# Two narrow query tiles of a causal attention transposed one behind the other in heads 0 to 6

## The chip, the cores and the metric

The kernel runs on one core of a Trainium2 chip. The metric is the device time in microseconds (us) of one execution. TensorE multiplies matrices, VectorE and ScalarE work on rows of 128 partitions, GpSimd and SyncE do little here but small vector work and the issue of transfers. In the profile's rows they are PE (its weight loads are PEld), DVE, ACT, POOL and SP.

## The reference, cut to what matters

The program is a two-layer trunk over 1024 frames of width 1024, in fp32, causal in chunks of 64 frames. Layer 1 is multi-scale retention. Layer 2, in which the change lies, is a latent attention of eight heads: queries, keys and values are projected from shared latents, each head takes

```python
scores = q_nope @ k_nope.T + q_rope @ k_rope.T     # 1024 x 1024, chunk-causal
p      = softmax(masked scores)
o      = p @ v                                     # 128 wide a head
h      = h + rmsnorm_post((silu(gate) * o) @ W_out)
```

Only the order in which the kernel works through query tiles is touched by the change; what is computed stays the same.

## The kernel before, in words

**Products.** TensorE multiplies fp32 data as two halves, so each product is three matmuls (mm3, L232 to L234: low by high, high by low, high by high). A result that is to be multiplied again is split when it leaves the accumulator: ScalarE copies the high part (L238), VectorE subtracts it from the result (L239). Each split frees its accumulator bank only when both have read it. There are two banks "acc" for products, two "r" for transposes, and two double banks "S" for scores.

**Tiles.** A head has eight query tiles i of 128 rows; tile i sees the first (i + 1) x 128 keys. They are taken from wide to narrow pairs: step 0 and 1 take b = 3 (tiles 6 and 7), steps 6 and 7 take b = 0 (tiles 0 and 1); qi is the place in the pair, i = 2b + qi. `score` (L1349) does ten matmuls, five for each piece of at most 512 keys (five in all up to 512), then VectorE writes the mask (L1376) and finds the maximum (L1379), ScalarE does the exponential with the row sum (L1382), and VectorE the reciprocal (L1383) and the product with it (L1384).

**Two steps late.** A tile is finished two steps after its scoring (LAG = 2): `finish` (L1387) first computes the values of the pair that is complete (`values`, L1419: 3 matmuls of 256 columns for each block of 128 keys, then a product with the gate on VectorE, L1430), and then transposes the tile's probabilities block by block on TensorE into an "r" bank (L1412) and splits them into pT. Only when the second tile of a pair (qi = 1) is transposed can the pair's values be computed, and that happens at the head of the next `finish`.

**Fill.** Between scoring and finishing, the next head's projections are placed as filler (`head_projections`, L1227): k blocks of 6, q blocks of 9 matmuls, and, for each even head, rotary query blocks with their rotation (L1280 to L1283 and L1292 on VectorE, eight transfers of L1288 on SyncE's queue, L1291 on ScalarE) and eight v blocks. So the odd heads 1, 3 and 5 carry the rotations of the heads 2, 4 and 6. In head 7 the filler is the output projection (its matmuls read thi, tlo, uhi and ulo; VectorE makes ulo, 128x1024, by the same split). How much filler a step takes is set by a count of columns: `done` sums what the step's own matmuls will stream, and filler is added until it reaches the step's share. A scheduler then sets the final order on each engine by estimated times.

**Blocks.** The probabilities p, their transposes pT and most other tiles come from one pool of 51 blocks of 128x1024 fp32 (`heap`), and a block that is given back is reused by the next that asks.

Of the kernel before, what the change touches and what calls it, by code (L numbers as in the profile page):

```python
# [18 lines left out]
P = 128  # L19
# [6 lines left out]
NH = 8  # L26
# [3 lines left out]
LAG = 2  # L30
# [22 lines left out]
class Units:  # L53
# [75 lines left out]
    def next(self):  # L129
        if not self.ready:  # L130
            self.prep()
        u = self.ready.popleft()
        self.fill()

        if self.at < len(self.order):
            n = self.pairs.index(self.order[self.at][0]) + 2
            while self.n_fetched < min(n, len(self.pairs)):
                self.fetch()
        return u
# [58 lines left out]
class Trunk:  # L198
# [1096 lines left out]
    def attention(self):  # L1295
        nc, I, heap = self.nc, self.I, self.heap
        self.heads = {}
        self.rq = []
        for half in range(2):
            r = heap.get("rq")  # L1300
            nc.sync.dma_start(r.rearrange("p (a t) -> p a t", a=2),
                              I["ropeq"][:, :, half * HALF:(half + 1) * HALF])
            self.rq.append(r)
        for _ in self.head_projections(0):
            pass
        self.pv = None
        open_tiles = deque()

        own = sum(5 * max(i + 1, 2) * P + (i + 1) * 2 * P + (i // 2 + 1) * 3 * 256 for i in range(NT))
        head, pair = 10 * 3 * HALF, 6 * 3 * HALF + 16 * 3 * 256  # L1310
        for h in range(NH):
            done = 0
            if h + 1 < NH:
                fill = self.head_projections(h + 1)
                share = (own + head + (pair if h % 2 else 0)) / 8
            else:
                self.prepare_out()
                fill = self.out_units()
                next(fill)
                share = (own + 32 * 3 * HALF) / 8  # L1320
            for step in range(8):
                b, qi = 3 - step // 2, step % 2
                s = self.score(h, b, qi)
                done += 5 * max(2 * b + qi + 1, 2) * P
                if self.pv is not None:
                    done += 6 * (self.pv[1] + 1) * 256
                if len(open_tiles) == LAG:
                    done += (2 * open_tiles[0][1] + open_tiles[0][2] + 1) * 2 * P
                while done < (step + 1.1) * share:
                    cost = next(fill, 0)  # L1330
                    if not cost:
                        break
                    done += cost
                if len(open_tiles) == LAG:
                    self.finish(open_tiles.popleft())
                open_tiles.append(s)
            if h + 1 < NH:
                for _ in fill:
                    pass
        self.scored = True  # L1340
        while open_tiles:
            self.finish(open_tiles.popleft())
            for _ in range(8):
                next(fill, 0)
        self.finish(None)
        for _ in fill:
            pass

    def score(self, h, b, qi):  # L1349

        nc, heap = self.nc, self.heap
        st = self.heads[h]
        mm = nc.tensor.matmul
        (qh, ql), (kh, kl), qr = st["q"], st["k"], st["pair"]["qr"][h % 2]
        rh, rl = self.krT
        i = 2 * b + qi
        qs = slice(i * P, (i + 1) * P)
        w = (i + 1) * P
        pieces = 1 if w <= HALF else 2
        used = w // pieces  # L1360
        n = max(used, 256)
        sc = self.bank("S", (P, 2, HALF))
        for c in range(pieces):
            ks = slice(c * n, (c + 1) * n)
            o = sc[:, c, :n]
            mm(o, ql[:, qs], kh[:, ks], start=True, stop=False)  # L1366
            mm(o, qh[:, qs], kl[:, ks], start=False, stop=False)  # L1367
            mm(o, qh[:, qs], kh[:, ks], start=False, stop=False)  # L1368

            mm(o, qr[:, qs], rl[:, ks], start=False, stop=False)  # L1370
            mm(o, qr[:, qs], rh[:, ks], start=False, stop=True)  # L1371
        if i == 1:
            heap.free(*st["q"], *st["k"])
            if h % 2:
                heap.free(*st["pair"]["qr"])
        nc.vector.memset(sc[0:64, pieces - 1, used - 64:used], -BIG)  # L1376
        view = sc[:, :pieces, :used]
        nm = self.small([P, 1], "nm", bufs=2)
        nc.vector.tensor_reduce(out=nm, in_=view, op=ALU.max, axis=AX.XY, negate=True)  # L1379
        p = heap.get("p")  # L1380
        sm = self.small([P, 1], "sm", bufs=2)
        nc.scalar.activation(p[:, :w].rearrange("p (a b) -> p a b", a=pieces), view, AF.Exp, bias=nm, accum_out=sm)  # L1382
        nc.vector.reciprocal(sm, sm)  # L1383
        nc.vector.tensor_scalar_mul(p[:, :w], p[:, :w], sm)  # L1384
        return h, b, qi, p
# [304 lines left out]
```

## Time and profile before

| | |
|---|---|
| runs of the kernel | 1257.58, 1258.1, 1259.8 us (median 1258.1) |
| the profiled execution | 1257.16 us, its span 1255.4 us |
| mean granted TensorE clock | 0.996 |
| TensorE, VectorE, ScalarE busy | 98 %, 83 %, 52 % of the span |
| attention (first score to the last head's last tile) | about 893 to 1205 us |

The profiled execution's time is 1.76 us more than its span, and 0.94 us below the median of the runs. A matmul's row has its start and its length; because matmuls overlap in the pipeline, the pace of TensorE is read from start to start, and a stall is a step from one start to the next that is longer than the pace of that kind of matmul. The table of busy times cannot show such stalls of a few tenths.

### The profile page before, as it was taken

The numbers are of one execution on the slowest core, as the hardware profiler recorded it, in microseconds if no ns is written. First come the engines' busy times: TensorE is split into PE (matmuls) and PEld (weight loads), VectorE is DVE, ScalarE is ACT, GpSimd is POOL, SyncE is SP. The second block draws the span as 40 slices with busy tenths as digits, with TensorE's granted clock in tenths as the row PEclk, the third lists the DMA queues.
The fourth block names the chain that finished last, engine by engine and source line by source line (L and its number), as shares of the span: only waits on it lengthen the run. The fifth ranks groups of instructions, "written<-read, shape, count | busy, mean of one in ns | idle before, by whom it ended". The sixth has DMA issues, their size and how long they took to land. (4 is left out here: it accounts for less than half of the span.)

```text
span 1255.4 us, 17688 instructions
## 1 busy us (share of the span) xinstructions
PE 1228.2 (98%) x6520; PEld 1058.8 (84%) x6520; DVE 1041.9 (83%) x1871; ACT 652.2 (52%) x1154; POOL 69.7 (6%) x86
## 2 busy tenths in 40 slices
PE   6999999999999999999999999999999999999997
PEld 5888888888888888888888789978888989898875
DVE  6878778898898988999998884675689888879787
ACT  7632125555564565655644867574354545545432
POOL 2000000000000000000000332100000000000001
PEclk9999999999999999999999999999999999999999
DMA  9248991232222322239799641032501010102454
GB/s 352 89 156 318 326 323 51 76 112 70 87 68 86 120 68 70 68 124 349 264 348 379 211 143 51 1 134 82 203 12 49 22 35 26 45 28 102 170 199 168
DMA packets 59640, 175.25 MB, mean 140 GB/s; under 512 B 7073, under 2 KB 16289, under 8 KB 59553
## 3 DMA queue, kind: packets, MB, share of 16 engines
q1 hardware_dynamic: 59552, 174.12, 39.3%
q8 instruction: 51, 0.84, 0.3%
q14 instruction: 37, 0.30, 0.1%
HBM read 124.81 MB, written 45.09 MB: 135 GB/s over the span
## 5 line engine op out<-in xcount | busy, mean ns | idle before, releaser
L232 PE MATMUL acc<-xhi,unit 128*128 128x512 f32 x560 | 220.5, 394 | 2.7 <-DVE u L414 2.3
L233 PE MATMUL acc<-xlo,unit 128*128 128x512 f32 x560 | 219.2, 391 | 0.0
L234 PE MATMUL acc<-xhi,unit 128*128 128x512 f32 x560 | 218.4, 390 | 0.0
L232 PEld LDWEIGHTS acc<-xhi,unit 128*128 128x128 f32 x560 | 105.4, 188 | 23.5 <-DVE u L414 2.7
L234 PEld LDWEIGHTS acc<-xhi,unit 128*128 128x128 f32 x560 | 105.2, 188 | 21.8
L233 PEld LDWEIGHTS acc<-xlo,unit 128*128 128x128 f32 x560 | 105.4, 188 | 19.3
L232 PE MATMUL acc<-vhi,xlo 128*128 128x512 f32 x224 | 88.9, 397 | 1.0 <-DVE xlo L239 1.0
L234 PE MATMUL acc<-vhi,xhi 128*128 128x512 f32 x224 | 88.0, 393 | 0.0
L233 PE MATMUL acc<-vlo,xhi 128*128 128x512 f32 x224 | 88.0, 393 | 0.0
L1382 ACT ACTIVATE p<-S,nm 128x896 f32<-128x896 f32 (+3 forms) x64 | 47.4, 741 | 63.5 <-DVE nm L1379 60.5
L238 ACT ACTIVATE unit<-wsum 128x512 fp32r<-128x512 f32 x80 | 50.4, 631 | 54.1 <-PE acc L234 44.7
L238 ACT ACTIVATE unit<-wraw 128x512 fp32r<-128x512 f32 x60 | 37.7, 630 | 56.3 <-DMA wraw<-in_w_in_a_dram 24.0
L238 ACT ACTIVATE vhi<-wv 128x1024 fp32r<-128x1024 f32 x28 | 29.3, 1060 | 64.8 <-PE acc L233 15.3
L239 DVE TENSOR_TENSOR unit<-wsum,unit 128x512 fp32r<-128x512 f32 x80 | 54.4, 684 | 8.5 <-ACT unit L238 8.4
L238 ACT ACTIVATE pT<-r 128x512 fp32r<-128x512 f32 (+2 forms) x96 | 44.4, 489 | 31.6 <-PE r L1412 31.4
L239 DVE TENSOR_TENSOR pT<-r,pT 128x512 fp32r<-128x512 f32 (+2 forms) x96 | 50.8, 550 | 6.1 <-ACT pT L238 5.8
L786 POOL TENSOR_TENSOR rg<-rg,mhalf 128x2 f32<-128x2 f32 x32 | 24.6, 768 | 547.3 <-DVE rg L785 527.1
L232 PEld LDWEIGHTS acc<-vhi,xlo 128*128 128x128 f32 x224 | 42.6, 190 | 10.0 <-DVE xlo L239 1.4
L238 ACT ACTIVATE thi<-wl 128x1024 fp32r<-128x1024 f32 x36 | 37.9, 1059 | 25.1 <-PE r L234 5.2
L232 PE MATMUL acc<-thi,slo 128*128 128x512 f32 x128 | 50.7, 397 | 0.0
L233 PE MATMUL acc<-tlo,shi 128*128 128x512 f32 x128 | 50.4, 395 | 0.1
L234 PE MATMUL acc<-thi,shi 128*128 128x512 f32 x128 | 50.4, 394 | 0.0
(327 smaller groups left out, 3467.2 us busy)
## 6 DMA issues: line engine op xcount, KB each, us to landing
wraw<-in_w_in_a_dram SPq DMA_DIRECT2D x32, 512.0 KB, 4.1
wv<-in_w_v_dram SPq DMA_DIRECT2D x28, 512.0 KB, 6.5
wl<-in_w_out_a_dram SPq DMA_DIRECT2D x28, 512.0 KB, 6.7
yl<-yd SPq DMA_DIRECT2D x28, 512.0 KB, 6.0
vd<-vo SPq DMA_DIRECT2D x32, 256.0 KB, 2.9
td<-wl SPq DMA_DIRECT2D x16, 512.0 KB, 3.3
vt<-vd SPq DMA_DIRECT2D x16, 512.0 KB, 3.2
yd<-yT SPq DMA_DIRECT2D x16, 512.0 KB, 4.7
```

The lines of the kernel that those rows point to most:

```text
L232: mm(ps, lhs[1], rhs[0], start=first, stop=False, skip_group_check=more)
L233: mm(ps, lhs[0], rhs[1], start=False, stop=False, skip_group_check=more)
L234: mm(ps, lhs[0], rhs[0], start=False, stop=last, skip_group_check=more)
L238: self.nc.scalar.activation(hi, src, AF.Copy)
L239: self.nc.vector.tensor_sub(lo, src, hi.bitcast(F32))
L786: nc.gpsimd.tensor_tensor(out=rg, in0=rg, in1=self.mhalf[:, 0:1].to_broadcast([P, 2]), op=ALU.pow)
L1382: nc.scalar.activation(p[:, :w].rearrange("p (a b) -> p a b", a=pieces), view, AF.Exp, bias=nm, accum_out=sm)
```

## The change

A function `due` says how many of the open tiles are finished in a step. In heads 0 to 6 the first tile (qi = 0) of the pairs b = 1 and b = 0 is held back one step, so three tiles are open, and in the next step both tiles of the pair are finished one directly behind the other. The count `done` sums over all tiles that are due. The values of pair b = 2 move from the sixth step to the seventh (counted from 0), those of b = 1 from step 0 to step 1 of the next head; in the step in which a tile is held, the pending values stay pending and are counted in `done` in both steps.

```diff
@@ -1324,14 +1324,15 @@
                 done += 5 * max(2 * b + qi + 1, 2) * P
                 if self.pv is not None:
                     done += 6 * (self.pv[1] + 1) * 256
-                if len(open_tiles) == LAG:
-                    done += (2 * open_tiles[0][1] + open_tiles[0][2] + 1) * 2 * P
+                due = self.due(open_tiles)
+                for o in list(open_tiles)[:due]:
+                    done += (2 * o[1] + o[2] + 1) * 2 * P
                 while done < (step + 1.1) * share:
                     cost = next(fill, 0)
                     if not cost:
                         break
                     done += cost
-                if len(open_tiles) == LAG:
+                for _ in range(due):
                     self.finish(open_tiles.popleft())
                 open_tiles.append(s)
             if h + 1 < NH:
@@ -1345,6 +1346,14 @@
         self.finish(None)
         for _ in fill:
             pass
+
+    def due(self, tiles):
+
+        if len(tiles) < LAG:
+            return 0
+        if len(tiles) == LAG and tiles[0][0] < NH - 1 and tiles[0][1] < 2 and tiles[0][2] == 0:
+            return 0
+        return len(tiles) - LAG + 1
 
     def score(self, h, b, qi):
 
```

The number of instructions on each engine stays the same. Lines behind the new function stand 9 lower than before (L1412 becomes L1421, L1430 becomes L1439).

On TensorE at the passage from an even head to an odd one, before: the end of a pair's values (acc_9795 from pT), then the one transpose of tile 0 (r_9812), then the scores of the widest tile, nine matmuls of a rotary query block (cqT by wlo and whi), the two transposes of tile 1 (r_9863), and the 320-column scores.

```order
4752 L234 MATMUL acc_9795<-pT_9713,v_9257 128x256
4753 L1412 MATMUL r_9812<-ident_136,p_9685 128x128
4754 L1366 MATMUL S_9816<-kT_9441,qT_9572 128x512
...
4763 L1371 MATMUL S_9816<-krT_7082,qr_8960 128x512
4764 L232 MATMUL acc_9853<-cqT_7523,wlo_9438 128x512
...
4772 L234 MATMUL acc_9853<-cqT_7525,whi_9437 128x512
4773 L1412 MATMUL r_9863<-ident_136,p_9732 128x128 x2
4774 L1366 MATMUL S_9868<-kT_9441,qT_9572 128x320
```

And after, at the same place:

```order
4763 L234 MATMUL acc_9836<-pT_9724,v_9283 128x256
4764 L1421 MATMUL r_9853<-ident_136,p_9674 128x128
4765 L1421 MATMUL r_9857<-ident_136,p_9699 128x128 x2
4766 L1375 MATMUL S_9862<-kT_9441,qT_9682 128x320
...
4775 L1380 MATMUL S_9862<-krT_7083,qr_8960 128x320
4776 L232 MATMUL acc_9832<-cqT_7523,wlo_9438 128x512
```

The three transposes of tiles 0 and 1 now stand together; the pair's values, the wide scores and the first three matmuls of the query block stand ahead of them, the block's other six behind the 320-column scores.

On VectorE a little further on in the same head, before: the tail of the second rotation (L1282, L1283), a half of the rotated query (L1292), and the splits of the next head's two k blocks (acc_9907, acc_9916).

```order
1441 L1282 TENSOR_TENSOR ra_9887<-acc_9853,rq_8438 64x512
1442 L1379 TENSOR_REDUCE nm_9880<-S_9868 128x1
1443 L1283 TENSOR_TENSOR ra_9887<-ra_9887 128x512
1444 L1292 TENSOR_TENSOR qr_9783<-rr_9836,qr_9783 64x512
1445 L239 TENSOR_TENSOR kT_9906<-acc_9907,kT_9905 128x512
...
1455 L239 TENSOR_TENSOR kT_9906<-acc_9916,kT_9905 128x512
1456 L1379 TENSOR_REDUCE nm_9959<-S_9947 128x1
```

And after:

```order
1446 L1283 TENSOR_TENSOR ra_9887<-ra_9887 128x512
1447 L1439 TENSOR_TENSOR gT_8404<-acc_9911,gT_8404 128x256
1448 L1292 TENSOR_TENSOR qr_9784<-rr_9815,qr_9784 64x512
1449 L239 TENSOR_TENSOR pT_9922<-r_9932,pT_9921 128x3x128
1450 L1385 MEMSET S_9938 64x64
1451 L239 TENSOR_TENSOR pT_9920<-r_9925,pT_9919 128x4x128
1452 L1388 TENSOR_REDUCE nm_9950<-S_9938 128x1
1453 L239 TENSOR_TENSOR kT_9906<-acc_9907,kT_9905 128x512
```

The first k block (acc_9907) is split eight places later than before, behind the gate product, two splits of transposed probabilities and the maximum of the next tile (nm_9950).

On TensorE late in head 7, before: the four last transposes of a tile with 512 keys (r_11867) and the one of the tile with 128 (r_11891), among output-projection matmuls (thi, tlo by uhi, ulo), and the first (L232) and second (L233) matmul of the values of b = 1 (acc_11874).

```order
5732 L1412 MATMUL r_11867<-ident_136,p_11717 128x128 x4
...
5736 L1412 MATMUL r_11891<-ident_136,p_11768 128x128
5737 L232 MATMUL acc_11863<-thi_11729,ulo_11839 128x512
5738 L232 MATMUL acc_11874<-pT_11807,v_10906 128x256
5739 L233 MATMUL acc_11863<-tlo_11730,uhi_11838 128x512
...
5745 L233 MATMUL acc_11863<-tlo_11734,uhi_11842 128x512
5746 L233 MATMUL acc_11874<-pT_11808,v_10905 128x256
```

And after:

```order
5729 L1421 MATMUL r_11857<-ident_136,p_11709 128x128 x4
5730 L1421 MATMUL r_11881<-ident_136,p_11762 128x128
5731 L232 MATMUL acc_11847<-thi_11482,ulo_11613 128x512
5732 L233 MATMUL acc_11847<-tlo_11483,uhi_11612 128x512
5733 L234 MATMUL acc_11847<-thi_11482,uhi_11612 128x512
5734 L232 MATMUL acc_11864<-pT_11801,v_10932 128x256
5735 L233 MATMUL acc_11864<-pT_11802,v_10931 128x256
```

Between the four transposes (of the tile with 512 keys) and the values' second matmul stood eleven output-projection matmuls, and now stand three.

## Rows read from the trace of the kernel before

**Rows 1.** The page's part 1: busy time of each engine, its share of the span, and its instructions.

```profile
PE 1228.2 (98%) x6520; PEld 1058.8 (84%) x6520; DVE 1041.9 (83%) x1871; ACT 652.2 (52%) x1154; POOL 69.7 (6%) x86
```

**Rows 2.** Table of stretches: from:to and length in us, then busy us (and instructions) of PE, PEld, DVE, ACT and POOL, the granted TensorE clock (1.00 is full speed), DMA share and GB/s. The stretch 1070 to 1110 is most of head 5, the last one is the end of the program.

```profile
1070.00:1110.00 40.00, 39.82 (x248) 35.47 (x248) 35.29 (x88) 19.24 (x46) 0.00 (x0) 1.00 0.11 27
...
1205.00:1256.00 51.00, 41.43 (x180) 33.19 (x178) 43.45 (x74) 17.72 (x39) 6.09 (x8) 0.93 0.49 173
```

**Rows 3.** VectorE's instructions from 893 to 1205 us by line and shape: out<-in, shapes, count, then busy us and mean ns of one, and idle time before them.

```profile
L239 DVE TENSOR_TENSOR pT<-r,pT 128x512 fp32r<-128x512 f32 x48 | 32.4, 685 | 5.1 <-ACT pT L238 5.0
...
L239 DVE TENSOR_TENSOR ulo<-gT,uhi 128x1024 fp32r<-128x1024 f32 x8 | 9.5, 1213 | 0.0
L239 DVE TENSOR_TENSOR pT<-r,pT 128x384 fp32r<-128x384 f32 x16 | 8.8, 547 | 0.9 <-ACT pT L238 0.8
...
L1379 DVE TENSOR_REDUCE nm<-S 128x1 f32<-128x768 f32 x8 | 7.4, 930 | 0.1
...
L1379 DVE TENSOR_REDUCE nm<-S 128x1 f32<-128x256 f32 x8 | 3.2, 398 | 0.0
```

**Rows 4.** TensorE in order of time in head 1 (start, us, instruction): a run of seven transposes and the first 384-column scores behind it.

```profile
949.72 0.93 PE L1412 MATMUL r<-ident,p 128*128 128x128 f32 x7
950.40 0.42 PE L1366 MATMUL S<-kT,qT 128*128 128x384 f32 x1
950.65 0.34 PE L1367 MATMUL S<-kT,qT 128*128 128x384 f32 x1
950.83 0.34 PE L1368 MATMUL S<-kT,qT 128*128 128x384 f32 x1
```

**Rows 5.** TensorE in order of time in head 5, from the end of the first rotary query block to the values of the next pair.

```profile
1078.08 0.39 PE L234 MATMUL acc<-cqT,whi 128*128 128x512 f32 x1
1078.31 0.28 PE L232 MATMUL acc<-pT,v 128*128 128x256 f32 x1
1078.42 0.28 PE L233 MATMUL acc<-pT,v 128*128 128x256 f32 x1
...
1087.25 0.60 PE L1412 MATMUL r<-ident,p 128*128 128x128 f32 x4
1087.98 0.50 PE L232 MATMUL acc<-ckvT,wlo 128*128 128x512 f32 x1
...
1090.70 0.34 PE L1371 MATMUL S<-krT,qr 128*128 128x384 f32 x1
1090.95 0.35 PE L232 MATMUL acc<-pT,v 128*128 128x256 f32 x1
...
1092.79 0.42 PE L1366 MATMUL S<-kT,qT 128*128 128x384 f32 x1
1093.15 0.50 PE L232 MATMUL acc<-cqT,wlo 128*128 128x512 f32 x1
1093.49 0.40 PE L233 MATMUL acc<-cqT,whi 128*128 128x512 f32 x1
...
1096.49 0.27 PE L232 MATMUL acc<-pT,v 128*128 128x256 f32 x1
1096.81 0.50 PE L1366 MATMUL S<-kT,qT 128*128 128x512 f32 x1
1097.15 0.39 PE L1367 MATMUL S<-kT,qT 128*128 128x512 f32 x1
```

**Rows 6.** VectorE in order of time: four instructions of head 5, and two late in head 7.

```profile
1078.51 0.69 DVE L1280 TENSOR_TENSOR ra<-acc,rq 128x512 f32<-128x512 f32 x1 [0.78 <-PE acc L234]
...
1084.38 0.69 DVE L1280 TENSOR_TENSOR ra<-acc,rq 128x512 f32<-128x512 f32 x1 [0.22 <-PE acc L234]
...
1090.11 0.69 DVE L239 TENSOR_TENSOR kT<-acc,kT 128x512 fp32r<-128x512 f32 x1
...
1093.82 0.67 DVE L239 TENSOR_TENSOR kT<-acc,kT 128x512 fp32r<-128x512 f32 x1
...
1182.96 0.42 DVE L1430 TENSOR_TENSOR gT<-acc,gT 128x256 f32<-128x256 f32 x1 [0.47 <-PE acc L234]
...
1190.18 2.35 DVE L239 TENSOR_TENSOR ulo<-gT,uhi 128x1024 fp32r<-128x1024 f32 x2
```

**Rows 7.** ScalarE in order of time in head 5: the exponential of the widest tile.

```profile
1084.26 1.12 ACT L1382 ACTIVATE p<-S,nm 128x1024 f32<-128x1024 f32 x1 [3.93 <-DVE nm L1379]
1085.27 0.19 ACT L1382 ACTIVATION_READ_ACCUMULATOR p<-S,nm 128x1 f32 x1
```

**Rows 8.** TensorE in order of time at the start and late in head 7.

```profile
1147.64 0.28 PE L233 MATMUL acc<-pT,v 128*128 128x256 f32 x1
1147.96 0.50 PE L232 MATMUL acc<-whi,ulo 128*128 128x512 f32 x1
...
1188.91 0.40 PE L234 MATMUL acc<-thi,uhi 128*128 128x512 f32 x1
1189.26 0.50 PE L232 MATMUL acc<-thi,ulo 128*128 128x512 f32 x1
...
1190.52 0.28 PE L233 MATMUL acc<-pT,v 128*128 128x256 f32 x1
...
1192.05 0.38 PE L1412 MATMUL r<-ident,p 128*128 128x128 f32 x2
1192.92 0.50 PE L232 MATMUL acc<-thi,ulo 128*128 128x512 f32 x1 [0.48 <-DVE gT L1430]
```

## The prediction

> **What bounds the kernel now.** I read the page's busy times first, then the table of stretches, then VectorE's instructions by shape, and last TensorE and VectorE in order of time at the places where the order changes. The busy times show TensorE at 98 % of the span, 1228.2 us, and VectorE next with 83 % [rows 1]. In the attention TensorE leaves 0.18 of 40 us free by busy time, at a granted clock of 1.00, while VectorE is busy 35.29 of 40 [rows 2]. So TensorE is the bound, and what an edit can win or lose there is time in which it waits. That is read from start to start, since a pipelined matmul counts as busy while the next one waits. The paces are 0.23 us for 512 columns and 0.11 to 0.12 for 256 [rows 5], 0.18 (0.175) for 384 [rows 4], and 0.147 for 320 columns as an estimate between those two. Seven transposes take 0.68 us to the next start, and the scores behind them 0.25 in place of 0.18 [rows 4]: (0.68 + 0.07) / 7 = 0.108 each. Two transposes alone would by this need 0.14 to the next start, and four 0.36.
>
> **What the bunching itself removes: nothing.** The same matmuls and transposes are issued, and the price of a change from transposes to matmuls is 0.07 us a run. In the seven heads the change joins 14 pairs of runs, so at most 14 x 0.07 = 1.0 us could go, if a transpose within a run were free of it; but that 0.07 is the rest of the last transpose's 0.108, not a fee for the change, so I cost it at 0, with bounds -1.0 and 0. VectorE and ScalarE keep one split for each tile, so nothing is saved there either. The rotation's eight transfers and the next head's weight loads keep their number on SyncE's queue; some are issued a few matmuls later or trade places. The cover is that what they bring is first needed in the next head; I cost them at 0 (bounds 0 and +0.3, an estimate from the 0.37 us of the largest stall in rows 5).
>
> What the change does is shift filler and values against VectorE's list, and TensorE's waits follow from where that list stands. Three places have a price.
>
> **A. Heads 3 and 5, behind the second rotary block.** Before: VectorE's list from the first L1280 (start 1078.51, released by the query block whose last matmul started at 1078.08) to the end of the second k split (1093.82 + 0.67 = 1094.49) is 31 instructions in 15.98 us [rows 6]. What needs that split is the values matmul at 1096.49, and 18.18 us after 1078.31; without the stalls in between, some 17.5 us of TensorE work [rows 5]. So the list is in time, and TensorE loses only small waits: 0.37 at 1087.98, 0.07 at 1090.95, 0.11 each at 1093.15 and 1093.49, 0.20 at 1096.81 and 0.11 at 1097.15, together 0.97 [rows 5].
>
> After: the list of 31 instructions from L1280 on now ends with the split of the first k block. In it the maximum over 768 keys (0.93) takes the place of one k split (0.69): +0.24 [rows 3, 6]. The 0.22 us for which VectorE waited ahead of the second L1280 goes, since that block is late now [rows 6]. A new wait comes: behind the maximum of the widest tile VectorE now has only the gate product (0.42 [rows 6]), one narrow split and two memsets, some 0.9 us, before the reciprocal, and ScalarE needs 1.12 us and a read-out for the exponential [rows 7]: 0.5 us. Sum 15.98 + 0.24 - 0.22 + 0.5 = 16.5, and 0.2 from 1078.31 to its start and 0.1 to the release: 16.8 us. Behind the rotation's matmul wait is the first matmul of the query block that needs this bank; between stand 31 matmuls of 512 columns (7.13), 18 of 256 (2.16), 18 transposes (1.94), 10 of 320 (1.47) and 15 of 384 (2.63), together 15.3 us. TensorE waits 16.8 - 15.3 = 1.5 us there. Queued behind that matmul are the transposes and scores of the next tiles, and on ScalarE the splits that need the rotated query's copies first; the list is then still late, up to 2.4 us in all if each of the next three splits adds what the stalls of before show (0.3). I take 2.0, against 0.97 before: **+1.0 a head, +2.0 for two** (bounds +1.0 and +2.9; if the list were in time, -1.9). Head 1 carries the same rotations beside head 0's filler, which has no place like this in its order; I take 0 (-1 to +1). The even heads have no rotations and VectorE has room: 0 (-0.5 to +0.5).
>
> **B. From head 6 to head 7.** There the last query block ends three matmuls later, and both query splits are wanted by head 7's first scores at once. From the end of tile 1's scores to those scores TensorE has 18 matmuls of 256, 7 + 3 transposes and 12 matmuls of 512: 2.16 + 1.08 + 2.76 = 6.0 us. VectorE has two splits of 128x1024 for the output projection (1.21 each), two of 512 columns (0.69), one of 384 (0.55) and a gate product (0.42): 4.8 us, and eight small ones (two masks, two maxima, two reciprocals, two products) of at most 0.40: 1.5 as an estimate [rows 3, 6]. That is 6.3 us, and the waits for ScalarE's copies ahead of four splits add 0 to 2; with 1.0 and 0.2 to the release TensorE waits 1.5 us, where before it lost 0.20 (1147.64 to 1147.96, less 0.12) [rows 8]: **+1.3** (bounds +0.3 and +2.3).
>
> **C. Late in head 7.** Before, the second values matmul of b = 1 starts at 1190.52 [rows 8], and the split that it needs ended when VectorE went on at 1190.18, 7.2 us after the gate product at 1182.96 [rows 6]: just in time. After, eight matmuls of 512 columns that stood ahead of it stand behind: 8 x 0.23 = 1.84 us earlier, 1188.7. VectorE's list ahead of that split holds one split of 1024 columns more (1.21 [rows 3]) and one sum of 512 less (0.69, as a split of that width): 1190.2 + 0.5 = 1190.7, so TensorE waits 2.0. Gone are the 0.12 at 1189.26 and the 0.73 at 1192.92 [rows 8], since the gate product that the latter waited for is then early: **+1.2** (bounds -0.8 and +1.6).
>
> Sum: 2.0 + 1.3 + 1.2 = 4.5 us. Behind head 7 TensorE stays the bound until shortly before the end (41.43 of 51 us busy, VectorE 43.45 in the last stretch [rows 2]), so I pass these on one to one. The sum stands against the profiled execution, 1257.16 us: 1261.7. That execution is 0.94 below the median of the runs; on the median it is 1262.6. I forecast 1262.2, between the two.
>
> **The rivals.**
> *Faster: VectorE is in time, and the old waits go.* If VectorE's list in heads 3 and 5 ends within the 15.3 us, the wait of A does not come, and the 0.97 us a head that TensorE lost around the narrow tiles goes with the order that made it; likewise 0.20 in B and 0.85 in C: -(1.94 + 0.20 + 0.85) = -3.0, so 1254.2 on the profiled execution and 1255.1 on the median. For it: VectorE's share is only 35.29 of 40 [rows 2], so over a whole head it catches up. Against it: 31 instructions must fit, and they took 15.98 us even without the new wait. It decides at a list 1.5 us shorter than I make it.
> *No change that can be measured: waits trade places.* A comes (+2.0), but B and C do not, and their old stalls go (-1.05): +1.0, 1258.2 on the profiled execution, 1259.1 on the median. For it: the old order's waits are of the same kind and size, a few tenths behind VectorE; the sums of A to C are differences of 0.5 to 2 us between lists of 6 to 17.
> *Slower by more: blocks come back later.* A tile held for a step keeps its block, and its pair's transposes ask for new ones in one go; if a transpose or a copy in each of the seven heads then waits as long as the largest stall of rows 5 (0.37), that adds 2.6: 1265.2. Against it: the order shows no instruction that has to wait for such a block before the splits of A.
> [...]
>
> **How the numbers follow.** My forecast 0.52, with its own range from 1260.3 (A at its lower bound, C at half) to 1264.8 (A and B at their upper ones); no change 0.27; faster 0.12; blocks 0.08; clock 0.01. What a measurement can tell from no change is about 0.2 %, 2.5 us, so 1255.6 to 1260.6 counts as the same. The forecast's lowest end falls in it (0.03 of its 0.52), and so does a little of the faster rival: faster 0.11, same 0.31, slower 0.58. The range 1256.0 to 1265.8 leaves out the lower part of the faster rival (0.08), the upper part of the blocks (0.03), the clock and the sum's far ends (some 0.08).
>
> **What would show it.** In the changed profile, TensorE's starts in heads 3 and 5 should have a step of 1 to 2 us ahead of a query block's first matmul (L232, cqT), with the k split of VectorE (L239) ending just before; VectorE's stretch from L1280 on should be gapless but for one wait of 0.5 at a reciprocal. B shows as a wait at head 7's first scores behind the q split or the transposes' split, C as a wait at the second values matmul behind the split of pT late in head 7. The granted clock should stay 1.00. I would be wrong if TensorE's steps in heads 3 and 5 add up to under 1 us a head, or if its pace near the joined transposes changed.

## The result, and the profile after

The changed kernel takes 1261.62 us (median of 15 runs, 1259.55 to 1262.64) against 1258.31 for the kernel before (15 runs on the same chips). The ratio is 1.0020, with a 95 % interval of 1.0014 to 1.0027: slower by 1.8 to 3.4 us. That is the way and about the size that was forecast (1262.2). The profiled executions lie further apart, 1262.64 against 1257.16 us, and that needs an explanation before any term is read.

The first lines are from TensorE in order of time, first of the kernel before, then of the changed one: the first score of head 0 and the last matmul of the program. (The table of the profile before puts the first score at about 893 us. That is where head 0's projections begin; the first score is at 909.10.)

```profile
909.10 0.37 PE L1366 MATMUL S<-kT,qT 128*128 128x448 f32 x1
...
1246.22 0.39 PE L234 MATMUL S<-whi,uhi 128*128 128x512 f32 x1
```

```profile
911.75 0.37 PE L1375 MATMUL S<-kT,qT 128*128 128x448 f32 x1
...
1252.32 0.39 PE L234 MATMUL S<-whi,uhi 128*128 128x512 f32 x1
```

Of the 5.4 us between the spans (1255.4 and 1260.8), 2.65 are there before the first score, in code that the change doesn't touch. The tables of stretches show where most of it arose (from:to and length, busy us of PE, PEld, DVE, ACT, POOL, the granted clock, DMA); first the kernel before, then the changed one:

```profile
826.00:836.00 10.00, 7.72 (x34) 6.07 (x33) 8.88 (x14) 7.96 (x17) 0.00 (x0) 1.00 0.31 107
```

```profile
826.00:837.00 11.00, 8.72 (x32) 6.78 (x31) 9.70 (x15) 8.70 (x18) 0.00 (x0) 0.84 0.29 98
```

TensorE stands still for 2.3 us in both. In the changed kernel's execution the granted clock is 0.84 in the stretch that holds the wait (six matmuls of 512 columns behind the wait started 0.43 us apart, in place of 0.23), in the other 1.00. Whether it falls there differs from execution to execution: it fell in 10 of the 14 profiles of this study, and the first score came between 908.35 and 912.44 us in them. So I compare from the first score to the last matmul: **337.12 us before, 340.57 after, +3.45**. What follows the last matmul takes 9.17 us before and 8.52 after, -0.65. Together +2.8, inside the interval of the timed runs.

The waits of TensorE in the changed kernel, as the view of waits sums them from 896 to 1250 us (engine, tile and line that waited, what it waited for: us, times, longest):

```profile
PE S L232 <- DVE yb L1580: 0.9, 1, 0.9
PE acc L232 <- DVE kT L239: 0.9, 2, 0.5
PE acc L233 <- DVE pT L239: 0.8, 1, 0.8
PE S L232 <- DVE yb L1563: 0.6, 1, 0.6
PE r L1421 <- DVE pT L239: 0.5, 1, 0.5
PE acc L232 <- ACT pT L238: 0.4, 1, 0.4
PE S L1375 <- DVE qT L239: 0.2, 1, 0.2
```

Nearly all are waits for VectorE, and each of the forecast places is among them: the k split (A), the transposes' split and the query split (B), the split of pT and the copy ahead of it (C). The two on yb, in the output projection, were not forecast.

Place A, in the changed kernel: TensorE in order of time in head 5 (to be held against [rows 5]).

```profile
1080.60 0.39 PE L234 MATMUL acc<-cqT,whi 128*128 128x512 f32 x1
1080.82 0.39 PE L1375 MATMUL S<-kT,qT 128*128 128x512 f32 x1
...
1083.54 0.39 PE L234 MATMUL acc<-cqT,whi 128*128 128x512 f32 x1
1083.96 0.39 PE L232 MATMUL acc<-pT,v 128*128 128x256 f32 x1
...
1085.49 0.49 PE L1421 MATMUL r<-ident,p 128*128 128x128 f32 x3
1085.74 0.39 PE L1375 MATMUL S<-kT,qT 128*128 128x320 f32 x1
1085.97 0.31 PE L1376 MATMUL S<-kT,qT 128*128 128x320 f32 x1
...
1096.79 0.34 PE L1380 MATMUL S<-krT,qr 128*128 128x384 f32 x1
1097.58 0.50 PE L232 MATMUL acc<-cqT,wlo 128*128 128x512 f32 x1 [0.45 <-DVE kT L239]
1097.91 0.40 PE L233 MATMUL acc<-cqT,whi 128*128 128x512 f32 x1
```

And VectorE there (to be held against [rows 6]):

```profile
1081.02 0.69 DVE L1280 TENSOR_TENSOR ra<-acc,rq 128x512 f32<-128x512 f32 x1 [0.76 <-PE acc L234]
...
1084.67 1.22 DVE L1388 TENSOR_REDUCE nm<-S 128x1 f32<-128x1024 f32 x1
...
1087.27 0.16 DVE L1392 RECIPROCAL sm<-sm 128x1 f32<-128x1 f32 x1 [0.38 <-ACT p L1391]
...
1089.44 0.68 DVE L1280 TENSOR_TENSOR ra<-acc,rq 128x512 f32<-128x512 f32 x1
...
1096.84 0.68 DVE L239 TENSOR_TENSOR kT<-acc,kT 128x512 fp32r<-128x512 f32 x1
```

The list from the first L1280 to the end of the first k split takes 1097.52 - 1081.02 = 16.50 us, gapless but for the 0.38 at the reciprocal, and the query block's first matmul starts right behind it, 0.79 after its predecessor in place of 0.175. Counting every step from start to start that is over 0.05 us longer than its pace, and summing by head from its first score to the next head's, TensorE lost 1.93 us in head 3 and 1.89 in head 5, against 1.12 and 1.26 before.

Places B and C: TensorE at the start of head 7 and late in it (to be held against [rows 8]).

```profile
1146.40 0.27 PE L1421 MATMUL r<-ident,p 128*128 128x128 f32 x1
1147.15 0.44 PE L1421 MATMUL r<-ident,p 128*128 128x128 f32 x2 [0.48 <-DVE pT L239]
1147.74 0.47 PE L1375 MATMUL S<-kT,qT 128*128 128x448 f32 x1 [0.16 <-DVE qT L239]
...
1191.42 0.40 PE L234 MATMUL acc<-thi,uhi 128*128 128x512 f32 x1
1192.21 0.38 PE L232 MATMUL acc<-pT,v 128*128 128x256 f32 x1 [0.39 <-ACT pT L238]
1193.35 0.39 PE L233 MATMUL acc<-pT,v 128*128 128x256 f32 x1 [0.76 <-DVE pT L239]
```

The joined transposes wait 0.64 for the split that frees an "r" bank, the scores behind them 0.40 for the query split. Late in head 7 the values of b = 1 wait 0.56 and 1.03.

The output projection behind head 7, first in the kernel before, then in the changed one:

```profile
1222.15 0.39 PE L233 MATMUL acc<-wlo,uhi 128*128 128x512 f32 x1
1222.72 0.50 PE L232 MATMUL S<-thi,ulo 128*128 128x512 f32 x1 [0.18 <-DVE yb L1554]
...
1232.38 0.39 PE L234 MATMUL acc<-whi,uhi 128*128 128x512 f32 x1
1232.70 0.50 PE L232 MATMUL S<-whi,ulo 128*128 128x512 f32 x1
```

```profile
1227.47 0.39 PE L233 MATMUL acc<-wlo,uhi 128*128 128x512 f32 x1
1228.50 0.50 PE L232 MATMUL S<-thi,ulo 128*128 128x512 f32 x1 [0.64 <-DVE yb L1563]
...
1237.70 0.39 PE L232 MATMUL acc<-whi,ulo 128*128 128x512 f32 x1
1239.03 0.50 PE L232 MATMUL S<-whi,ulo 128*128 128x512 f32 x1 [0.94 <-DVE yb L1580]
```

Steps of 0.80 and 1.10 us beyond the pace, where the same places lost 0.34 and 0.10 before: VectorE reads the "S" banks of finished blocks (yb) later than TensorE wants them back.

### The profile page after: what moved, and what is told of

Read it like the earlier page. It is cut to its first block, busy times and chain, and to the rows that moved or that the text cites. A ratio compares the mean times of both kernels' runs of the same rounds, so it can differ in the third digit from the quotient of the medians.

```text
span 1260.8 us, 17669 instructions
## 1 busy us (share of the span) xinstructions
PE 1231.2 (98%) x6520; PEld 1059.4 (84%) x6520; DVE 1040.4 (83%) x1871; ACT 652.6 (52%) x1154; POOL 68.0 (5%) x86
## 5 line engine op out<-in xcount | busy, mean ns | idle before, releaser
L232 PE MATMUL acc<-xhi,unit 128*128 128x512 f32 x560 | 221.1, 395 | 2.5 <-DVE u L414 2.3
L233 PE MATMUL acc<-xlo,unit 128*128 128x512 f32 x560 | 219.7, 392 | 0.0
L232 PEld LDWEIGHTS acc<-xhi,unit 128*128 128x128 f32 x560 | 105.7, 189 | 23.4 <-DVE u L414 2.7
L233 PEld LDWEIGHTS acc<-xlo,unit 128*128 128x128 f32 x560 | 105.8, 189 | 19.6
L232 PE MATMUL acc<-vhi,xlo 128*128 128x512 f32 x224 | 89.2, 398 | 1.0 <-DVE xlo L239 1.0
L233 PE MATMUL acc<-vlo,xhi 128*128 128x512 f32 x224 | 88.2, 394 | 0.0
L232 PEld LDWEIGHTS acc<-vhi,xlo 128*128 128x128 f32 x224 | 42.7, 191 | 10.1 <-DVE xlo L239 1.4
L233 PE MATMUL acc<-tlo,shi 128*128 128x512 f32 x128 | 50.6, 396 | 0.4 <-DVE tlo L239 0.4
L232 PE MATMUL acc<-thi,slo 128*128 128x512 f32 x128 | 50.6, 396 | 0.0
```

Source lines behind the costliest of these rows:

```text
L232: mm(ps, lhs[1], rhs[0], start=first, stop=False, skip_group_check=more)
L233: mm(ps, lhs[0], rhs[1], start=False, stop=False, skip_group_check=more)
```

## The experiments

All runs are measured alike: the ratio to the kernel before on the same chip, then from the profile the time from the first score to the last matmul, and the stalls (us) of head 1, heads 3 and 5, head 6, and head 7 with the output projection, counted as above. The profile's columns carry one execution each, and the kernel before was profiled once. The experiments ran on two chips. From the first score to the end of the program, a profile's difference from the one profile of before lies 1.3 to 1.9 us below the difference of the timed medians in the four runs on the one chip (once, late, b0, b1), and 0.1 to 1.9 us above it in the eight on the other. So a difference of under 2 us in the third column is no proof of a difference in time; the ratios are. The stalls of heads whose order is unchanged repeat within 0.1 us (heads 1 to 5 of h6 and of before).

| run | ratio (95 %) | first score to last matmul | head 1 | 3, 5 | 6 | 7 and output |
|---|---|---|---|---|---|---|
| before | 1 | 337.12 | 1.3 | 1.1, 1.3 | 0.5 | 2.1 |
| the change | 1.0020 (1.0014 to 1.0027) | 340.57 | 0.5 | 1.9, 1.9 | 1.4 | 4.1 |
| once | 0.9995 (0.9986 to 1.0003) | 336.03 | 0.8 | 0.7, 0.7 | 0.9 | 2.0 |
| late | 1.0042 (1.0030 to 1.0055) | 342.15 | 2.8 | 1.8, 1.9 | 1.0 | 4.2 |
| b0 | 1.0035 (1.0021 to 1.0049) | 340.68 | 0.7 | 1.9, 2.0 | 1.0 | 4.2 |
| b1 | 1.0000 (0.9992 to 1.0009) | 336.09 | 1.2 | 1.1, 1.0 | 0.3 | 1.9 |
| h6 | 1.0001 (0.9992 to 1.0009) | 339.79 | 1.3 | 1.1, 1.3 | 0.4 | 4.9 |
| h0to5 | 1.0005 (0.9996 to 1.0014) | 338.42 | 0.5 | 1.9, 1.9 | 0.9 | 2.4 |
| early | 1.0044 (1.0032 to 1.0056) | 343.20 | 0.9 | 1.0, 1.0 | 2.0 | 6.2 |
| pool_after | 1.0029 (1.0020 to 1.0039) | 342.43 | 1.8 | 2.1, 2.2 | 1.6 | 3.9 |
| nosum_after | 1.0020 (1.0010 to 1.0029) | 342.05 | 1.6 | 2.3, 1.8 | 1.5 | 4.2 |
| nosum_before | 1.0009 (0.9998 to 1.0019) | 340.18 | 2.0 | 2.0, 2.0 | 0.3 | 2.9 |
| h7once | 1.0009 (1.0000 to 1.0018) | 338.56 | 0.5 | 1.9, 1.9 | 1.3 | 2.2 |
| best2 | 0.9985 (0.9977 to 0.9994) | 336.49 | 0.7 | 0.6, 0.7 | 0.8 | 2.5 |

**Is it the joining, or the count?** The change does two things: it holds and joins tiles, and in doing so it counts the pending values in two steps, so that filler is placed later. The first pair takes them apart. `once` keeps the joining and drops the second counting:

```diff
-                if self.pv is not None:
-                    done += 6 * (self.pv[1] + 1) * 256
                 due = self.due(open_tiles)
+                if self.pv is not None and due:
+                    done += 6 * (self.pv[1] + 1) * 256
```

> Tiles held and joined as in the change, but the pending values are counted once, in the step in which they run, so the filler isn't late. Filler theory: the first k block of heads 3 and 5 is whole before the transposes again, its split comes early in VectorE's list, and the step of 0.61 us ahead of the query block's matmul goes; stalls of heads 3 and 5 near 1.0 us each (1.03 before, 1.62 in the change), time 1258 to 1259.5. Rival, the joining and holding itself costs: stalls stay at 1.6 a head, time 1261 to 1262.

`late` is the kernel before, with nothing joined, and the change's count:

```diff
                 if len(open_tiles) == LAG:
-                    done += (2 * open_tiles[0][1] + open_tiles[0][2] + 1) * 2 * P
+                    i = 2 * open_tiles[0][1] + open_tiles[0][2]
+                    if open_tiles[0][0] == NH - 1 or i > 3:
+                        done += (i + 1) * 2 * P
+                    elif i % 2:
+                        done += (2 * i + 1) * 2 * P + 6 * (i // 2 + 2) * 256
```

> The kernel before with the change's count alone: each tile is finished two steps after its scoring as before, no transposes joined, but the filler is counted as in the change and so comes late. Filler theory: a step of 0.5 to 0.7 us ahead of the query block's matmul in heads 3 and 5, 1.5 us of stalls a head, time 1260 to 1262. Rival, the joining itself: stalls 1.0 a head, time 1258 to 1259.

The joining alone, with the values counted once, costs nothing that can be measured (1258.19 us, 0.9995). (`once` is not the old filler to the matmul: in the first step of a head it counts 3328 columns less than before, the 3072 of the values and the 256 of the held tile, and makes them up in the second.) And the count alone costs more than the whole change (1264.08 us, 1.0042; more than I expected). In `late`, TensorE waits in head 5 for the same k split, at the values matmul that is next in line there (TensorE in order of time):

```profile
1099.75 0.40 PE L234 MATMUL acc<-cqT,whi 128*128 128x512 f32 x1
1100.92 0.39 PE L232 MATMUL acc<-pT,v 128*128 128x256 f32 x1 [0.78 <-DVE kT L239]
```

So the second count, and the late filler that it makes, is the cause. Given the late filler, joining even seems to help: ratio 1.0042 without it, 1.0020 with it, though the two were measured at different times.

**Which pair?** In `due`, `tiles[0][1] < 2` becomes `tiles[0][1] == 0` (`b0`) or `tiles[0][1] == 1` (`b1`).

> Only the pair b = 0 is joined in heads 0 to 6, b = 1 as before. Filler theory: heads 3 and 5 start with the change's order, so 1.6 us of stalls each there; with B and C as in the change 1260.5 to 1262. If it is the pair b = 1 that costs: 1258 to 1259.

> Only the pair b = 1 is joined in heads 0 to 6, b = 0 as before. Filler theory: heads 3 and 5 start with the order of before, stalls 1.0 us each, and the passage into head 7 is the old one (0.3 us); time 1258 to 1259.5. If it is the pair b = 1 that costs: 1261 to 1262.

All of it comes with b = 0, whose held tile makes the first filler of the next head late (1262.97 us, more than I expected); the pair b = 1 is free (1258.67 us). Its late filler falls at the end of a head, where the rest is issued anyway; that this is why it does no harm is read from the code.

**Which head?** In `due`, `tiles[0][0] < NH - 1` becomes `== NH - 2` (`h6`) or `< NH - 2` (`h0to5`).

> Tiles held and joined in head 6 alone, all else as before. If the late filler at the passage into head 7 makes the waits there, late in head 7 and in the output projection behind it: the steps of 0.56 and 1.02 us ahead of the values of b = 1 and those of 0.80 and 1.10 us in the output projection are here, heads 3 and 5 have their old 1.0 us, time 1261 to 1262.5. If these waits come from the whole change (five heads' drift): the old steps, time 1258 to 1259.

> Tiles held and joined in heads 0 to 5, not in head 6. By the same theory: heads 3 and 5 have 1.6 us, head 1 0.5 us, and the passage into head 7, late head 7 and the output projection have the old steps (0.3, 0.95, 0.45): time 1258.3 to 1259.3. If the drift of all heads counts: 1260.5 to 1262.

By the profiles the two add up: +2.67 and +1.30 from the first score to the last matmul, less 0.83 and 0.41 behind it, 2.7 together, where the whole change has 2.8. The waits late in head 7 and in the output projection are in `h6`, as expected (the second one in the output projection is even larger there, 1.93 us). The wait at the start of head 7 is not; it is in `h0to5` (a step of 0.80), since the held tile of head 5 delays the filler of head 6, which holds the query block. There I had expected it the other way round. The timed runs do not bear the sum out: 1.0001 and 1.0005, together 0.0006, against 1.0020 for the whole change. `h6` took 1259.49 us where I expected 1261 to 1262.5, and its ratio is at most 1.0009 where its profile has 1.8 us, 0.15 %; `h0to5` took 1260.30 where I expected at most 1259.3. In these sessions the kernel before itself had a median of 1259.57 us, 1.26 more than beside the change, so much of that gap may be the one profile of before that stands for all; it is not settled, and how the loss is shared between the heads is shown in the traces alone.

`h7once` tests the same from the other end: the changed kernel, with the pending values counted once in head 7 alone.

```diff
-                if self.pv is not None:
-                    done += 6 * (self.pv[1] + 1) * 256
                 due = self.due(open_tiles)
+                if self.pv is not None and (due or h < NH - 1):
+                    done += 6 * (self.pv[1] + 1) * 256
```

> The changed kernel, but in head 7 alone the pending values are counted once, so that only head 7's own filler (the output projection) isn't late. If the waits late in head 7 and in the output projection behind it (2.3 us more than before in the profile) come from that count: they go back to 1.8 us, while the passage from head 6 (1.3) and heads 3 and 5 (1.9 each) keep theirs: 1259 to 1260.5. If they come from the passage itself or from head 6's order: unchanged, 1261 to 1262.5.

The waits late in head 7 and in the output projection are back at 2.2 us, the others stay, and the time is 1260.16 us (1.0009, 1.0000 to 1.0018): by the ratios these waits are worth about half of the loss, though the interval overlaps a little with that of the whole change, and they come from head 7's own filler. At the passage TensorE still waits as in the change (in order of time):

```profile
1147.56 0.44 PE L1421 MATMUL r<-ident,p 128*128 128x128 f32 x2 [0.49 <-DVE pT L239]
1148.15 0.47 PE L1375 MATMUL S<-kT,qT 128*128 128x448 f32 x1 [0.16 <-DVE qT L239]
```

**Is late the only wrong side?** `early` moves the filler of the kernel before the other way:

```diff
-                if self.pv is not None:
+                if self.pv is not None and (h == 0 or step):
                     done += 6 * (self.pv[1] + 1) * 256
```

> The kernel before with the filler moved the other way: in step 0 the pending values are not counted (3072 columns less, where the change counts 3072 more in step 1), no tile held. If lateness is what costs, earlier filler costs nothing here or wins up to 1 us (k splits in time, stalls of heads 3 and 5 at most 1.0): 1257 to 1259. If any shift from the tuned order costs: 1260 or more.

In heads 1 to 5 it is as expected: 0.9, 1.0 and 1.0 in the odd heads, all a little under the kernel before. But heads 6 and 7 lose 8.2 us where they lost 2.5, and the time is 1265.29 us. The two largest steps are these, 1.63 and 1.81 us beyond the pace (TensorE in order of time):

```profile
1133.72 0.39 PE L233 MATMUL acc<-pT,v 128*128 128x256 f32 x1 [1.47 <-DVE pT L239]
...
1149.00 0.50 PE L1366 MATMUL S<-kT,qT 128*128 128x512 f32 x1 [1.57 <-ACT p L1382]
```

The first waits for VectorE's split. The second waits for an exponential of ScalarE, which has three copies of 1.06 us each ahead of it there. So earlier is not better as such: at the passage into head 7 both engines have the output projection's long splits as well, and the moved filler meets them. My expectation for the whole was wrong, and the time is in the range of the rival that any shift from the old order costs. In that wide form the rival is out too: `once`, `b1` and `best2` shift the order and cost nothing.

**Is it the length of VectorE's list?** Two trials took work off it. `pool_after` gives the rotation's sum and the zeroing of pT blocks to GpSimd in the changed kernel (`nc.vector.tensor_add(a, a, b)` and the `memset` in `finish` become `nc.gpsimd...`).

> The changed kernel with the rotation's sum (L1283 of before, 128x512) and the zeroing of pT blocks given from VectorE to GpSimd, which is idle there. Theory that VectorE's list of 31 instructions is what the wait of 0.61 us in heads 3 and 5 hangs on: 1.4 us and some memsets off the list, so that step goes, stalls of heads 3 and 5 0.5 to 1.0 us, time 1259.5 to 1261 (the waits of head 7 stay). Rival, it is ScalarE's copies or the bank itself: the step stays at 0.6, time 1261 to 1262. If GpSimd takes time from VectorE on shared memory: slower than 1262.

It is slower, 1263.03 us (1.0029). VectorE and then GpSimd in order of time in head 5 of that run:

```profile
1092.82 1.61 DVE L1393 TENSOR_SCALAR p<-p,sm 128x640 f32<-128x640 f32 x1
```

```profile
1092.15 1.80 POOL L1283 TENSOR_TENSOR ra<-ra 128x512 f32<-128x512 f32 x1 [5.27 <-DVE ra L1282]
```

GpSimd needs 1.80 us here for a sum that VectorE does in 0.68 (mean), and while it runs, VectorE's product of 640 columns takes 1.61 us, where the mean is 0.55 in the changed kernel. So 1.06 of the 1.4 us came back at once, and the run can't decide. `nosum_after` and `nosum_before` leave the sum out, so their rotated queries are not the reference's.

```diff
-        nc.vector.tensor_add(a, a, b)
```

> The changed kernel without the rotation's sum (L1283 of before: left out, so the rotated queries of the second to eighth head and what follows from them aren't the reference's). Theory that the length of VectorE's list is what TensorE waits for in heads 3 and 5: 1.2 to 1.4 us come off the list without any other engine taking them over, the step of 0.62 us ahead of the query block's matmul goes, stalls of heads 3 and 5 fall from 1.9 to at most 1.0 us each; head 7 and the output projection keep theirs; 1259 to 1261. Rival, the bank's or ScalarE's own order: the step stays.

> The same left out of the kernel before, to see how much of its own stalls in heads 1, 3 and 5 (1.3, 1.1, 1.3 us) hang on the same list. Theory: they fall to 0.3 to 0.8 each, 1256 to 1258; the gain is smaller than in the changed kernel, since the list of before was in time. Rival, equal gain or none in both: the change's late k split isn't what costs.

The step that I had named is gone in `nosum_after`, but the head does not gain (2.3 and 1.8 us), and in the kernel before the stalls grow to 2.0 a head. VectorE and TensorE in head 5 of `nosum_after`:

```profile
1095.00 0.67 DVE L239 TENSOR_TENSOR kT<-acc,kT 128x512 fp32r<-128x512 f32 x1
1095.69 0.69 DVE L1291 TENSOR_TENSOR qr<-rr,qr 64x512 fp32r<-64x512 f32 x1
```

```profile
1100.58 0.39 PE L234 MATMUL acc<-cqT,whi 128*128 128x512 f32 x1
1101.61 0.39 PE L1374 MATMUL S<-kT,qT 128*128 128x256 f32 x1 [0.64 <-ACT p L1390]
```

The k split is in time now, but the planner has used the shorter list to take a half of the rotated query (needed only in the next head) ahead of the next tile's maximum, and the next scores wait 0.80 us for an exponential. So the step hung on that list, as I said, but the time of a head does not follow from its length: less work for VectorE gave no gain in either kernel (1261.48 us, 1.0020, and 1260.66 us, 1.0009, where I expected 1259 to 1261 and 1256 to 1258). That is the outcome of the rival by which the late k split is not what costs, and that part of my theory falls. My reading is that after any edit the scheduler makes the order anew, by its estimated times, and another instruction is late; the rows show the new order and the new wait, but no run holds the order fixed, so whether a shorter list alone would win time is open.

**A version that is faster than both.** It is joined, counted once, and in head 6 only the pair b = 1. To the edit of `once` it adds, in `due`:

```diff
-        if len(tiles) == LAG and tiles[0][0] < NH - 1 and tiles[0][1] < 2 and tiles[0][2] == 0:
+        if len(tiles) == LAG and tiles[0][2] == 0 and (tiles[0][1] == 1 and tiles[0][0] < NH - 1 or tiles[0][1] == 0 and tiles[0][0] < NH - 2):
```

> Tiles joined with the values counted once in heads 0 to 5, and in head 6 only the pair b = 1. Theory: filler nowhere late, so stalls of heads 3 and 5 at 0.7 us as in the run that counts once, and the passage to head 7 as in the run that joins b = 1 alone: first score to last matmul 335.5 to 336.5 us against 337.1 before, time 1256.5 to 1258.5. Rival, no gain from this: 1258 to 1259.5.

1258.07 us, ratio 0.9985 (0.9977 to 0.9994): 0.8 to 2.9 us faster than the kernel before. From the first score to the last matmul it has 336.49 us, 0.6 less than before; most of what it wins is in heads 3 and 5 (0.6 and 0.7 against 1.1 and 1.3).

## Why the prediction was right

The forecast was 1262.2 us and the likeliest case, slower by waits behind VectorE at A, B and C, is what the traces show. That the second count makes the loss is shown by `once` and `late`; that it makes it through these waits is read from the traces, and the timed runs confirm a share only for head 7 (`h7once`). Point by point:

- **The bunching itself, 0**: right. `once` joins the same tiles, counts the values once and has a ratio of 0.9986 to 1.0003.
- **A, +2.0 in heads 3 and 5: measured +1.44** (1.93 + 1.89 - 1.12 - 1.26). The list was put at 16.5 us and took 16.50 (it has 32 instructions in both kernels, not 31; the wait at the reciprocal was 0.38 of the 0.5); the work in front of the query block was put at 15.3 us, and from 1080.82 to where the matmul could have started (1096.97) there are 16.15 us, less 0.81 of earlier stalls. Of the wait of 1.5, which I put at that one matmul, 0.62 stood there and the 0.81 had been lost on the way, such as the 0.30 at 1083.96; so the sign that I named, a step of 1 to 2 us at that place, did not come, and the sum over the head did. What was off is the old side: I counted 0.97 of stalls before from the steps in [rows 5], and the head as a whole had 1.1 to 1.3.
- **Head 1, 0 within -1 to +1: measured -0.8** (1.29 to 0.46).
- **B, +1.3: measured +1.0** (1.29, being the 0.64 and 0.40 shown above and 0.25 at the query block, against 0.30).
- **C, +1.2: measured +0.9** (1.89 against 0.95). VectorE's list from the gate product to the gating split was put 0.5 us longer than before; what VectorE did there:

```profile
1185.79 0.42 DVE L1439 TENSOR_TENSOR gT<-acc,gT 128x256 f32<-128x256 f32 x1 [2.38 <-PE acc L234]
...
1192.62 0.88 DVE L239 TENSOR_TENSOR pT<-r,pT 128x512 fp32r<-128x512 f32 x2
```

 From 1185.79 to 1193.3 are 7.5 us, against 7.2 before [rows 6].
- **The output projection: the step that failed.** "I pass these on one to one" held the rest of the program for unchanged. Its filler order changed with head 7's count, and it lost 2.2 us in place of 0.75, +1.5; behind the last matmul 0.65 came back.

The sum of my terms, 4.5, is above the 2.8 from the traces: A, B and C were 1.1 too high together, head 1 won 0.8, the output projection lost 0.8 net, and what is left, in the other heads and in steps under 0.05 us, is a gain of about 0.5. Errors of both signs; that the total lies so near owes something to that. The range of the case does not come out of its terms either: with A at its lower bound and C at half the forecast falls to 1260.6, not 1260.3, and with A and B at their upper bounds it rises to 1264.1, not 1264.8. Neither changes which case the result falls in.

Of the rivals, "VectorE is in time" is out by the rows of A. "Waits trade places" is in part true: head 1 gained 0.8, head 5 lost 0.6. For the rival of the blocks I saw no wait that a block would explain, though no run held a block back, so it is not tested. The clock, to whose fall the forecast gives 0.01, stayed at 1.00 (912 to 1207 us): the three joined transposes take 0.25 us to the next start and the 320-column scores behind run 0.15 us apart, as before; behind a run of eight, the 384-column scores run 0.18 us apart. Neither of the two traces shows a fall of the clock behind transposes.

## What to carry to other kernels

When an edit changes a count that a planner reads, test the count and the edit apart before you explain the time: here the joining was free, and the second counting of one product cost all of the loss. Where two engines are 98 and 83 % busy, read at each place which list the busy one waits for, from its first released instruction to the one that frees the bank; at A the distance in work on both sides gave the lag of the list, 1.5 us, to 0.1 us, though it was spread over several matmuls. And expect the stage behind the edit to be replanned too: compare it before you pass a shift on unchanged.

## What the runs showed of the hardware

Giving VectorE's work to the idle GpSimd slowed VectorE: a product of 640 columns took 1.61 us beside GpSimd's 1.80 us sum, against a mean of 0.55. Two more instructions of VectorE that began while such a sum ran were slow too: another product of 640 columns (1.48 us) and a difference of 64x512 (1.29 us against a mean of 0.69). All three ended 0.4 to 0.6 us after the sum's end, the first one 0.48. By the means of their groups, the eight products took 0.80 us against 0.55 in the changed kernel, and the sixteen differences 0.73 against 0.69. The maxima over 1024 keys took 1.22 us in the mean in both, and the one that ran beside the 1.30 us sum of head 5 took 1.22 as well. Why some are slowed and others are not, no run here shows. The eight sums take 1.55 us in the mean on GpSimd against 0.68 on VectorE, 2.3 times.

The granted clock after one and the same wait of 2.3 us, ahead of the attention, was 1.00 in one execution and 0.84 over the stretch in another, where six matmuls of 512 columns in a row started 0.43 us apart in place of 0.23. The first scores of the 14 profiles lie up to 4.1 us apart, so differences of that size between two single profiles of this kernel say nothing until the stretch in front is taken off; and up to 2 us can remain even then.
